# Seven-product down projections for twelve of the 22 chunks in both FFNs of a hybrid encoder block

## The chip, the cores and the metric

The kernel runs on one core of a Trainium2 chip. The metric is device time in microseconds, the median of several runs. In the profile PE is the matmul engine, PEld its weight load, DVE, ACT and POOL are the vector, scalar and GpSimd engines, and SP issues most DMAs.

## What is computed

One encoder layer on 512 tokens of width 1024, in float32: an FFN, a mixer of two attention groups, and a second FFN, each with RMS norms around it. The change touches the FFNs alone:

```python
def swiglu(h, w_gu, w_down):
    gate, up = jnp.split(h @ w_gu, 2, axis=-1)
    return (jax.nn.silu(gate) * up) @ w_down

f = swiglu(rms_norm(h, ffn1_pre_g[l]), ffn1_w_gu[l], ffn1_w_down[l])
h = h + 0.5 * rms_norm(f, ffn1_post_g[l])
...
f = swiglu(rms_norm(h, ffn2_pre_g[l]), ffn2_w_gu[l], ffn2_w_down[l])
h = h + 0.5 * rms_norm(f, ffn2_post_g[l])
```

The hidden width is 2816, which is 22 chunks of 128. `ffn1_w_down` is 2816 x 1024.

## The kernel before

Every float32 operand is split in two fp32r parts, a high one (an ACT copy) and a low one (a DVE or POOL subtraction): `split`, line 333. A product is three matmuls, high x high, high x low and low x high (`mm3`, line 351). The low part's subtraction has two inputs from SBUF.

`ffn` (line 392) has two stages. The first makes the gated hidden values chunk by chunk. Its first chunks are plain (`gate_up`); from chunk `direct` on, `winograd` (line 460) makes gate and up together by a form of seven products in place of eight, with operand sums on POOL and DVE (`operands`, line 434) and a recombination on DVE and ACT. It uses matmuls of 256 columns. Each chunk of 128 x 512 gated values goes to DRAM (`gd`).

The second stage is the down projection: out[token, 1024] is a sum over 22 chunks. The 512 tokens are four tiles of 128, and the 1024 output columns two halves, so the sums fill all eight PSUM banks of 128 x 512, bank 2n + hf. For each chunk `load_w` fetches 128 rows of `w_dn` (512 KB) and splits them, `load_gT` (line 530) fetches the chunk's gated values (256 KB) and splits them into a place of `slots`, and `down` (line 539) runs for each tile three matmuls of 512 columns into each of two banks: 24 matmuls per chunk. Chunks 0 and 1 are done two tiles at a time, chunks 2 to 17 in the loop at line 557, and the last four (`TAIL`) tile by tile, so that each tile's norm and residual addition (`on_tile`) run beside the next tile's matmuls. The four residual loads (`SP.dma_start(h[n], resid(n))`, lines 555 and 556) stand ahead of that loop. For the first FFN, tile n's work also issues what the mixer needs: `mid1` (line 703) and `after1` (line 710).

The order of all instructions on each engine is set by `Plan` (lines 47 to 239). It records every operation with the ranges that it reads and writes, places them in a list schedule by costs of its own, forwards and backwards several times, and emits the best order. `tc.keep_in_program_order` then holds it. This is why nearly every instruction of the profile stands at line 238.

The tile `m32` holds plain float32 data (loads, scratch `scr`, the residual `hall`); its name in the profile is `m`. The tile `memr` holds the split parts.

Of the kernel before, what the change touches and what calls it, by code (L numbers as in the profile page):

```python
# [15 lines left out]
ALU = mybir.AluOpType  # L16
AX = mybir.AxisListType

P = 128
D = 1024  # L20
S = 512
NT = S // P
KD = D // P
FF = 2816
NFC = FF // P
# [4 lines left out]
TAIL = 4  # L30
# [216 lines left out]
def hybrid_block(ctx, tc, A, out):  # L247
# [16 lines left out]
    def bank(i, n=512):  # L264
        return psum[:, i * 512 : i * 512 + n]
# [39 lines left out]
    def reg(o, n):  # L305
        assert R0 + o + n <= NCOL - N32
        return mem[:, R0 + o : R0 + o + n]
# [40 lines left out]
    def mm(ps, a, b, start, stop):  # L348
        return PE.matmul(ps, r_(a), r_(b), start=start, stop=stop, skip_group_check=True)
# [42 lines left out]
    def ffn(w_gu, w_dn, gpost, on_tile, L, first, resid, mid_tile=None, rs=None):  # L392
# [133 lines left out]

        slots, last_w = ([reg(o, 1024) for o in x] for x in (L["slots"], L["last_w"]))
        gT = {}

        def load_gT(c):  # L530
# [8 lines left out]
        def down(c, n, w, first, last, hfs=(0, 1)):  # L539
            t = slice(n * P, (n + 1) * P)  # L540
            for (a, b) in ((0, 0), (0, 1), (1, 0)):
                for hf in hfs:
                    mm(bank(2 * n + hf), gT[c][a][:, t], w[b][:, hf * 512 : hf * 512 + 512],
                       first and a + b == 0, last and a == 1)

        g = load_g(gpost)
# [4 lines left out]
        for ns in ((0, 1), (2, 3)):  # L551
            for c in range(2):
                for n in ns:
                    down(c, n, w01[c], c == 0, False)
        for n in range(NT):
            SP.dma_start(h[n], resid(n))
        for c in range(2, NFC - TAIL):
            w = load_w(w_dn[c * P : (c + 1) * P, :])
            load_gT(c)
            for n in range(NT):  # L560
                down(c, n, w, c == 0, False)
        ws = []
        for c in range(NFC - TAIL, NFC):
            ws.append(load_w(w_dn[c * P : (c + 1) * P, :], to=last_w if c == NFC - 1 else None))
            load_gT(c)
# [156 lines left out]
    def scale(k):  # L722
# [13 lines left out]
        "order": lambda c: 1 if c < 8 else (c + 1) % 2,  # L736
        "slots": [1024 * i for i in range(7)] + [8192 + 1024 * i for i in range(6)]
        + [26624 + 1024 * i for i in range(4)] + [7168] + [14336 + 1024 * i for i in range(4)],
        "last_w": (26624, 27648),
    }  # L740
# [416 lines left out]
    def after2(n, t):  # L1157
# [15 lines left out]
        "order": lambda c: c % 2,  # L1173
        "slots": [19456 + 1024 * i for i in range(7)] + [4096 + 1024 * i for i in range(15)],
        "last_w": (19456, 20480),
    }
# [70 lines left out]
```

## Time and profile before

| what | before |
|---|---|
| median of 3 runs | 946.56 us (946.36 to 946.84) |
| the profiled execution | 949.77 us |
| its span from first to last instruction | 948.0 us |
| PE busy | 937.1 us (99%) |
| DVE busy | 693.6 us (73%) |
| ACT busy | 477.9 us (50%) |
| POOL busy | 289.6 us (31%) |

The busy times are shares of the span. An engine's share is a mean over stages that differ: the gate and up stages, the mixer and the down stages each have their own.

### The profile page before, as it was taken

What the parts mean: (1) busy time and instruction counts of PE and PEld (TensorE: products, weight loads), DVE (VectorE), ACT (ScalarE), POOL (GpSimd) and SP (SyncE); (2) the same over time, 40 slices, a digit from 0 to 9 for tenths busy, and PEclk for the clock granted to TensorE, in tenths of its full rate; (3) what the DMA queues carried; (4) which work ended last, traced back from release to release, by engine and by line L of the source; (5) the groups of instructions that cost most, each with busy time, mean ns of one, the idle gap of its engine ahead of it and who ended that gap; (6) DMA issues with size and microseconds to landing.
All of it is one profiled execution on the core that took longest, in us unless ns stands there. A gap on an engine that the chain in (4) does not pass through costs nothing. (4 is left out here: it accounts for less than half of the span.)

```text
span 948.0 us, 15333 instructions
## 1 busy us (share of the span) xinstructions
PE 937.1 (99%) x5930; PEld 850.5 (90%) x5930; DVE 693.6 (73%) x977; ACT 477.9 (50%) x850; POOL 289.6 (31%) x233
## 2 busy tenths in 40 slices
PE   9999999999999999999999999999999999999996
PEld 8789999999888888889988888999999999988885
DVE  5799999998622376587687678999989899642224
ACT  5545455544521353588677767654445444432122
POOL 0005575660000013222452323227566672000000
PEclk9999999999999999999899999999999999999999
DMA  9634444449762356113371115254444337843312
GB/s 271 219 129 157 149 131 134 134 150 283 238 152 88 122 189 132 46 55 68 103 175 47 45 45 178 92 191 141 136 133 139 141 112 230 265 158 91 91 43 89
DMA packets 61897, 130.11 MB, mean 137 GB/s; under 512 B 21888, under 2 KB 23808, under 8 KB 61824
## 3 DMA queue, kind: packets, MB, share of 16 engines
q1 hardware_dynamic: 60672, 127.30, 43.0%
q0 software_dynamic: 1008, 1.84, 1.1%
q8 instruction: 46, 0.75, 0.3%
q14 instruction: 27, 0.22, 0.1%
q10 hardware_dynamic: 144, 0.00, 0.0%
HBM read 109.45 MB, written 17.83 MB: 134 GB/s over the span
## 5 line engine op out<-in xcount | busy, mean ns | idle before, releaser
L238 PE MATMUL psum<-memr 128*128 128x256 f32 (+2 forms) x5572 | 914.5, 324 | 0.4 <-ACT memr L238 0.2
L238 PEld LDWEIGHTS psum<-memr 128*128 128x128 f32 x5572 | 808.5, 191 | 78.6 <-ACT memr L238 2.1
L238 DVE TENSOR_TENSOR memr<-m,memr 128x1024 fp32r<-128x1024 f32 (+3 forms) x313 | 367.0, 1196 | 132.6 <-ACT memr L238 132.5
L238 POOL TENSOR_TENSOR m<-m 128x512 f32<-128x512 f32 (+5 forms) x193 | 252.1, 1321 | 567.6 <-DVE m L238 397.4
L238 ACT CAST memr<-m 128x1024 fp32r<-128x1024 f32 (+1 forms) x321 | 265.1, 841 | 277.2 <-PE psum L238 167.8
L238 DVE TENSOR_TENSOR m<-psum,m 128x512 f32<-128x512 f32 (+3 forms) x176 | 109.7, 625 | 36.0 <-ACT m L238 22.7
L238 DVE TENSOR_TENSOR memr<-psum,memr 128x512 fp32r<-128x512 f32 (+3 forms) x116 | 68.0, 603 | 24.8 <-ACT memr L238 23.8
L238 ACT CAST memr<-psum 128x512 fp32r<-128x512 f32 (+2 forms) x124 | 62.6, 524 | 41.8 <-PE psum L238 31.8
L238 PE MATMUL psum<-m 128*128 128x128 f32 (+1 forms) x358 | 59.3, 285 | 3.1 <-DVE m L238 3.1
L238 PEld LDWEIGHTS psum<-m 128*128 128x128 f32 x358 | 47.9, 162 | 11.1 <-DVE m L238 3.6
L238 ACT ACTIVATE m<-psum 128x256 f32<-128x256 f32 (+2 forms) x62 | 27.4, 444 | 53.5 <-PE psum L238 33.0
L238 ACT ACTIVATE m<-m 128x256 f32<-128x256 f32 (+3 forms) x80 | 36.9, 461 | 27.2 <-DVE m L238 26.9
L238 DVE TENSOR_TENSOR psum<-psum,m 128x512 f32<-128x512 f32 (+1 forms) x78 | 42.8, 571 | 6.4 <-PE psum L238 5.4
L238 ACT COPY m<-psum 128x256 f32<-128x256 f32 (+3 forms) x72 | 30.9, 432 | 24.6 <-PE psum L238 23.0
L238 DVE SCALAR_TENSOR_TENSOR m<-m 128x512 f32<-128x512 f32 (+1 forms) x36 | 33.7, 968 | 4.9 <-POOL m L238 4.3
L238 DVE TENSOR_TENSOR m<-m 128x512 f32<-128x512 f32 (+2 forms) x42 | 33.2, 799 | 0.7
L238 ACT ACTIVATE m<-psum,m 128x512 f32<-128x512 f32 x40 | 27.0, 688 | 10.3 <-DVE m L238 7.3
L238 ACT ACTIVATE memr<-m 128x512 fp32r<-128x512 f32 (+2 forms) x28 | 21.0, 760 | 13.2 <-DVE m L238 9.9
L238 POOL TENSOR_TENSOR memr<-m,memr 128x1024 fp32r<-128x1024 f32 x9 | 21.6, 2409 | 14.6 <-ACT memr L238 13.0
L238 POOL CAST memr<-memr 64x512 fp32r<-64x512 f32 x8 | 5.9, 740 | 51.4 <-DVE memr L238 51.4
L238 DVE TENSOR_SCALAR m<-m 128x1 f32<-128x1 f32 (+1 forms) x36 | 6.4, 179 | 20.6 <-ACT m L238 10.7
L238 DVE TENSOR_REDUCE m<-psum 128x1 f32<-128x512 f32 x32 | 21.2, 682 | 0.1
(24 smaller groups left out, 95.6 us busy)
## 6 DMA issues: line engine op xcount, KB each, us to landing
m<-in_ffn_w_gu SPq DMA_DIRECT2D x86, 512.0 KB
m<-in_ffn_w_down SPq DMA_DIRECT2D x44, 512.0 KB
gd<-m SPq DMA_DIRECT2D x44, 256.0 KB
m<-gd SPq DMA_DIRECT2D x44, 256.0 KB
m<-in_x SPq DMA_DIRECT2D x8, 512.0 KB
m<-in_w_qk SPq DMA_DIRECT2D x8, 512.0 KB
h<-m SPq DMA_DIRECT2D x8, 512.0 KB
m<-in_w_out SPq DMA_DIRECT2D x8, 512.0 KB
```

Of the source, the lines that this page charges most:

```text
L238: r = getattr(self.engines[eng], op)(*a, **k)
```

## The change

Chunks 3 to 8 and 12 to 17 of each FFN go two chunks and two token tiles at a time. With two chunks as the inner split, two tiles as rows and two column halves as columns, each such block is a 2 x 2 by 2 x 2 product, done with seven products in place of eight. Three pairs of chunks make a group (`down_pairs`).

- `weight_operands` makes the seven right-hand operands of a pair of chunks: four DVE subtractions of 128 x 512, then the split of seven 128 x 512 blocks (four ACT copies and four DVE subtractions).
- `gate_operands` makes the seven left-hand operands for two chunks and two tiles: two loads of 128 x 256, four POOL operations of 128 x 128, and splits of 384 and of 512 columns.
- The seven products of one token pair need seven banks (0 to 2 keep their running sums, 4 to 7 are fresh), and the two tiles' own four sums are the ones in banks 0 to 3. So the other token pair's four sums are copied to SBUF (`keep`, which is the residual's place `hall`), the first pair runs, eight DVE additions recombine it into `keep` and the other pair's sums come back into banks 0 to 3; then the second pair runs and is recombined in PSUM, and the first pair's sums go into banks 4 to 7. The table `at` notes that the two pairs have changed places.
- The residual loads move behind the loop, since `hall` is in use until then. The places of the split gated values (`slots`) become few and are reused, where before each chunk had its own.

```diff
-        slots, last_w = ([reg(o, 1024) for o in x] for x in (L["slots"], L["last_w"]))
+        plain = [c for c in range(NFC - TAIL) if not any(p <= c < p + 6 for p in L["pairs"])]
+        slots = {c: reg(L["slots"][0] + i % 3 * 1024, 1024) for i, c in enumerate(plain)}
+        slots |= {c: reg(L["slots"][1] + (c - NFC + TAIL) * 1024, 1024) for c in range(NFC - TAIL, NFC)}
         gT = {}
+        at = {(n, hf): 2 * n + hf for n in range(NT) for hf in range(2)}
...
-                    mm(bank(2 * n + hf), gT[c][a][:, t], w[b][:, hf * 512 : hf * 512 + 512],
+                    mm(bank(at[n, hf]), gT[c][a][:, t], w[b][:, hf * 512 : hf * 512 + 512],
...
+        keep = [hall[:, 512 * i : 512 * i + 512] for i in range(8)]
+        raw_w = Ring([scr[:, 1024 * i : 1024 * i + 1024] for i in range(3)])
+
+        def weight_operands(i, c):
+
+            m = reg(L["w_at"][i], 7168)
+            r0 = raw_w.get()
+            r1 = raws.get() if i == 1 else raw_w.get()
+            for r, k in ((r0, c), (r1, c + 1)):
+                SP.dma_start(r, w_dn[k * P : (k + 1) * P, :])
+            b11, b12, b21, b22 = r0[:, :512], r0[:, 512:], r1[:, :512], r1[:, 512:]
+            part = lambda i, j: (m[:, 512 * i : 512 * j], m[:, 3584 + 512 * i : 3584 + 512 * j])
+            DVE.tensor_tensor(b12, b12, b11, ALU.subtract)
+            split(*part(0, 1), b11)
+            split(*part(1, 3), r1)
+            DVE.tensor_tensor(b22, b22, b12, ALU.subtract)
+            DVE.tensor_tensor(b11, b22, b11, ALU.subtract)
+            DVE.tensor_tensor(b21, b21, b22, ALU.subtract)
+            split(*part(3, 5), r0)
+            split(*part(5, 7), r1)
+            return {k: part(i, i + 1) for i, k in enumerate(("11", "21", "22", "T3", "T1", "T4", "T2"))}
+
+        def gate_operands(i, c, n):
+
+            m = [reg(o, 1024) for o in L["g_at"][i]]
+            raw = half_g.get()
+            for k in range(2):
+                SP.dma_start(raw[:, 256 - 256 * k : 512 - 256 * k], gdr[c + k][:, n * P : (n + 2) * P])
+            a12, a22, a11, a21 = (raw[:, P * k : P * k + P] for k in range(4))
+            part = lambda i, j: (m[0][:, P * i : P * j], m[1][:, P * i : P * j])
+            split(*part(0, 3), raw[:, :384])
+            POOL.tensor_tensor(a21, a11, a21, ALU.subtract)
+            POOL.tensor_tensor(a22, a22, a21, ALU.subtract)
+            POOL.tensor_tensor(a12, a12, a22, ALU.subtract)
+            POOL.tensor_tensor(a11, a22, a11, ALU.add)
+            split(*part(3, 7), raw)
+            return {k: part(i, i + 1) for i, k in enumerate(("12", "22", "11", "S4", "S2", "S1", "S3"))}
+
+        def down_pairs(c0):
+
+
+            x, y = sorted((at[n, 0] // 4, n) for n in (0, 2))
+            x, y = x[1], y[1]
+            gs = Ring(range(4))
+            W = [weight_operands(i, c0 + 2 * i) for i in range(3)]
+            for i in range(4):
+                ACT.copy(keep[i], bank(4 + i))
+            for n in (x, y):
+                for i in range(3):
+                    G = gate_operands(gs.get(), c0 + 2 * i, n)
+                    for b, l, r in ((0, "12", "21"), (1, "S4", "22"), (2, "22", "T4"), (4, "11", "11"),
+                                    (5, "S2", "T2"), (6, "S3", "T3"), (7, "S1", "T1")):
+                        mm3(bank(b), G[l], W[i][r], b > 3 and i == 0, i == 2)
+                to = [keep[6], keep[0], keep[1], keep[2]] if n == x else [bank(i) for i in range(4)]
+                p1, u2, u3, u4, u5 = (keep[i] for i in (4, 5, 7, 4, 5))
+                back = (lambda i: ACT.copy(bank(i), keep[i])) if n == x else lambda i: None
+                add = lambda o, a, b: DVE.tensor_tensor(o, a, b, ALU.add)
+                ACT.copy(p1, bank(4))
+                add(u2, bank(5), p1)
+                add(to[0], bank(0), p1)
+                back(0)
+                add(u3, bank(6), u2)
+                add(u4, bank(7), u2)
+                add(to[1], bank(1), u4)
+                back(1)
+                add(u5, bank(7), u3)
+                add(to[2], bank(2), u3)
+                back(2)
+                add(to[3], bank(3), u5)
+                back(3)
+            for i, k in enumerate((6, 0, 1, 2)):
+                ACT.copy(bank(4 + i), keep[k])
+            for i in range(4):
+                at[y + i // 2, i % 2], at[x + i // 2, i % 2] = i, 4 + i
...
-        for n in range(NT):
-            SP.dma_start(h[n], resid(n))
-        for c in range(2, NFC - TAIL):
+        c = 2
+        while c < NFC - TAIL:
+            if c in L["pairs"]:
+                down_pairs(c)
+                c += 6
+                continue
             w = load_w(w_dn[c * P : (c + 1) * P, :])
             load_gT(c)
             for n in range(NT):
                 down(c, n, w, c == 0, False)
+            c += 1
+        for n in range(NT):
+            SP.dma_start(h[n], resid(n))
         ws = []
         for c in range(NFC - TAIL, NFC):
-            ws.append(load_w(w_dn[c * P : (c + 1) * P, :], to=last_w if c == NFC - 1 else None))
+            ws.append(load_w(w_dn[c * P : (c + 1) * P, :]))
...
+        "pairs": (3, 12), "w_at": (9216, 16384, 23552), "g_at": [(3072 + 2048 * i, 4096 + 2048 * i) for i in range(3)] + [(0, 1024)],
+        "slots": (0, 12288),
...
+        "pairs": (3, 12), "w_at": (0, 7168, 23552), "g_at": ((14336, 15360), (16384, 17408), (18432, 22528), (19456, 20480)),
+        "slots": (19456, 0),
```

Three places of the planned order show it. The first is PE in the first FFN's down stage, before (-) and now (+); the 128 x 128 rows are transposes of the next stage.

```order
 L238 MATMUL psum<-memr 128x256 x1344
-L238 MATMUL psum<-memr 128x512 x492
-L238 MATMUL psum<-m_63 128x128 x8
-L238 MATMUL psum<-memr 128x512 x24
+L238 MATMUL psum<-memr 128x512 x460
+L238 MATMUL psum<-m_63 128x128 x8
+L238 MATMUL psum<-memr 128x512 x20
```

36 matmuls of 512 columns are gone (in the second FFN one run of 528 becomes 492), and the first transposes stand four matmuls nearer the end of the stage.

The second is DVE in the same stage. Before, between the last gate and up chunk and the first tile's norm there are only low parts (`memr<-m,memr`): 512 columns for gated values, 1024 for weights.

```order
L238 TENSOR_TENSOR memr<-m_63,memr 128x1024
L238 TENSOR_TENSOR memr<-m_63,memr 128x512 x4
L238 TENSOR_TENSOR memr<-m_63,memr 128x1024
L238 TENSOR_TENSOR memr<-m_63,memr 128x512 x3
L238 TENSOR_TENSOR memr<-m_63,memr 128x1024 x17
L238 TENSOR_TENSOR m_63<-psum,m_63 128x512
```

Now the first group's weight operands stand there, subtractions in `m` and low parts of three sets in one run:

```order
L238 TENSOR_TENSOR m_63<-m_63 128x512 x4
L238 TENSOR_TENSOR memr<-m_63,memr 128x1024 x2
L238 TENSOR_TENSOR memr<-m_63,memr 128x512
L238 TENSOR_TENSOR m_63<-m_63 128x512 x3
L238 TENSOR_TENSOR memr<-m_63,memr 128x384
L238 TENSOR_TENSOR memr<-m_63,memr 128x1024 x2
L238 TENSOR_TENSOR m_63<-m_63 128x512
L238 TENSOR_TENSOR memr<-m_63,memr 128x512
L238 TENSOR_TENSOR memr<-m_63,memr 128x1024
L238 TENSOR_TENSOR m_63<-m_63 128x512 x3
L238 TENSOR_TENSOR memr<-m_63,memr 128x512
L238 TENSOR_TENSOR memr<-m_63,memr 128x1024 x2
```

The addition from PSUM that begins the first recombination follows these rows directly.

The third is POOL between the first FFN's gate and up stage (its 128 x 512 rows) and the mixer (64 x 128).

```order
 L238 TENSOR_TENSOR m_63<-m_63 128x512 x56
-L238 TENSOR_TENSOR m_63<-m_63 128x1 x5
+L238 TENSOR_TENSOR m_63<-m_63 128x128 x48
+L238 TENSOR_TENSOR m_63<-m_63 128x1 x8
+L238 TENSOR_TENSOR m_63<-m_63 64x128 x3
+L238 TENSOR_TENSOR m_63<-m_63 128x256
```

The 48 operations of 128 x 128 are the two groups' gate operands; POOL had none in the down stage.

## Rows read from the trace of the kernel before

**Rows 1.** The page's busy line; then PE's waits: us, times, longest.

```profile
PE 937.1 (99%) x5930; PEld 850.5 (90%) x5930; DVE 693.6 (73%) x977; ACT 477.9 (50%) x850; POOL 289.6 (31%) x233
...
PE psum L238 <- DVE m L238: 3.1, 4, 1.1
```

**Rows 2.** Busy time by stretch, clock, DMA: gate and up twice, down.

```profile
core 0: us, PE busy (x) PEld busy (x) DVE busy (x) ACT busy (x) POOL busy (x), PEclk, DMA share, GB/s
100.00:200.00 100.00, 100.00 (x835) 100.00 (x835) 97.74 (x102) 51.60 (x81) 64.98 (x42) 1.00 0.41 135
640.00:800.00 160.00, 160.00 (x1336) 160.00 (x1335) 148.25 (x164) 76.93 (x128) 102.61 (x64) 1.00 0.44 144
840.00:900.00 60.00, 60.00 (x266) 49.70 (x265) 14.19 (x12) 11.55 (x12) 0.00 (x0) 1.00 0.32 97
```

**Rows 3.** Groups by shape, 840 to 900 us, down: busy, mean ns, idle before.

```profile
L238 PE MATMUL psum<-memr 128*128 128x512 f32 x266 | 60.5, 389 | 0.0
...
L238 DVE TENSOR_TENSOR memr<-m,memr 128x1024 fp32r<-128x1024 f32 x11 | 13.5, 1226 | 45.2 <-ACT memr L238 45.2
...
L238 DVE TENSOR_TENSOR memr<-m,memr 128x512 fp32r<-128x512 f32 x1 | 0.7, 694 | 0.4 <-ACT memr L238 0.4
```

**Rows 4.** Timeline, gate and up: start, length, engine; DVE back to back.

```profile
194.69 0.68 DVE L238 TENSOR_TENSOR m<-psum,m 128x512 f32<-128x512 f32 x1
...
195.29 1.21 DVE L238 TENSOR_TENSOR memr<-m,memr 128x1024 fp32r<-128x1024 f32 x1
...
196.43 1.02 DVE L238 TENSOR_TENSOR psum<-psum,m 128x512 f32<-128x512 f32 x2
```

**Rows 5.** Groups by shape, whole run, DVE: subtraction inside SBUF.

```profile
L238 DVE TENSOR_TENSOR m<-m 128x512 f32<-128x512 f32 x26 | 17.6, 687 | 0.5
```

**Rows 6.** Groups by shape, whole run, POOL.

```profile
L238 POOL TENSOR_TENSOR m<-m 128x256 f32<-128x256 f32 x20 | 17.9, 898 | 42.0 <-DVE m L238 40.7 <-ACT memr L238 1.0
L238 POOL TENSOR_TENSOR m<-m 64x128 f32<-64x128 f32 x16 | 7.9, 494 | 3.4 <-DVE m L238 2.7
```

**Rows 7.** Groups by shape, DVE, 100 to 200, then 640 to 800 us.

```profile
L238 DVE TENSOR_TENSOR memr<-m,memr 128x512 fp32r<-128x512 f32 x32 | 45.5, 1473 | 0.0
L238 DVE TENSOR_TENSOR memr<-m,memr 128x1024 fp32r<-128x1024 f32 x20 | 27.7, 1386 | 0.0
L238 DVE TENSOR_TENSOR m<-psum,m 128x512 f32<-128x512 f32 x30 | 20.5, 682 | 2.3 <-ACT m L238 1.2
...
L238 DVE TENSOR_TENSOR memr<-m,memr 128x512 fp32r<-128x512 f32 x51 | 61.9, 1245 | 0.0
L238 DVE TENSOR_TENSOR memr<-m,memr 128x1024 fp32r<-128x1024 f32 x32 | 43.7, 1372 | 0.0
```

**Rows 8.** Groups by shape, whole run, ACT.

```profile
L238 ACT CAST memr<-m 128x1024 fp32r<-128x1024 f32 x164 | 170.0, 1047 | 189.8 <-PE psum L238 139.1 <-POOL m L238 19.8 <-DVE m L238 16.2
L238 ACT CAST memr<-m 128x512 fp32r<-128x512 f32 x152 | 93.3, 620 | 85.9 <-PE psum L238 27.2 <-POOL m L238 22.4 <-DMA m<-gd 15.4
...
L238 ACT ACTIVATE psum<-m 128x1024 f32<-128x1024 f32 x8 | 8.2, 1027 | 6.6 <-DMA m<-in_x 5.4 <-DVE m L238 1.1
L238 ACT COPY m<-psum 128x512 f32<-128x512 f32 x13 | 7.4, 586 | 1.4 <-PE psum L238 0.8 <-DVE memr L238 0.5
```

**Rows 9.** Busy by stretch (columns as in rows 2); PE's groups in 233 to 235.

```profile
215.00:230.00 15.00, 15.00 (x127) 15.00 (x126) 12.49 (x19) 6.31 (x12) 0.00 (x0) 1.00 1.01 285
320.00:346.00 26.00, 26.00 (x116) 21.52 (x116) 15.40 (x19) 11.88 (x18) 1.66 (x3) 1.00 0.59 201
...
L238 PE MATMUL psum<-memr 128*128 128x512 f32 x2 | 0.6, 397 | 0.0
```

**Rows 10.** Timeline, end of the first gate and up stage: its last addition.

```profile
236.17 0.69 DVE L238 TENSOR_TENSOR m<-psum,m 128x512 f32<-128x512 f32 x1 [0.51 <-ACT m L238]
```

**Rows 11.** Timeline, second down stage: a weight load, and a later copy.

```profile
832.47 0.33 SPq L238 DMA_DIRECT2D m<-in_ffn_w_down  x1
...
836.78 1.57 ACT L238 CAST memr<-m 128x512 fp32r<-128x512 f32 x2 [2.37 <-DMA m<-gd]
```

More of the change, by code (lines that the diff above doesn't have):

```diff
@@ L736, in hybrid_block @@
         "order": lambda c: 1 if c < 8 else (c + 1) % 2,
-        "slots": [1024 * i for i in range(7)] + [8192 + 1024 * i for i in range(6)]
-        + [26624 + 1024 * i for i in range(4)] + [7168] + [14336 + 1024 * i for i in range(4)],
-        "last_w": (26624, 27648),
+        "pairs": (3, 12), "w_at": (9216, 16384, 23552), "g_at": [(3072 + 2048 * i, 4096 + 2048 * i) for i in range(3)] + [(0, 1024)],
+        "slots": (0, 12288),
     }
@@ L1173, in hybrid_block @@
         "order": lambda c: c % 2,
-        "slots": [19456 + 1024 * i for i in range(7)] + [4096 + 1024 * i for i in range(15)],
-        "last_w": (19456, 20480),
+        "pairs": (3, 12), "w_at": (0, 7168, 23552), "g_at": ((14336, 15360), (16384, 17408), (18432, 22528), (19456, 20480)),
+        "slots": (19456, 0),
     }
```

## The prediction

> **What bounds the kernel now.** I began with the page's busy line and the waits. PE is busy for 937.1 of 948.0 us, and its longest waits for another engine are four for DVE, 3.1 us in all [rows 1]. So a matmul that is taken away is worth its full time, as long as the other engines keep up. Next come the stretches [rows 2]: in the gate and up stage (100 to 200 us, 640 to 800 us) PE and DVE are both nearly full, in the down stage (840 to 900 us) PE is full while DVE works 14.19 us of 60 and POOL not at all. The change spends that free DVE time to save PE time. The question is whether there is enough of it in the right places.
>
> **What it removes.** For two chunks and two token tiles, eight products of three matmuls become seven. Six chunks are 144 matmuls of 512 columns, now 126; there are two such groups in each FFN, so 4 x 18 = 72 go, as the order of PE shows (492 to 460 plus 24 to 20 in FFN 1, 528 to 492 in FFN 2). In the down stage 266 of them fill 60.00 us [rows 2, 3], 0.2256 us each: 72 x 0.2256 = **16.2 us less**. The granted clock is 1.00 in these stretches, so none of it is slow-clock time.
>
> **What it adds to DVE.** DVE's own durations overlap at their ends: starts at 194.69, 195.29 and 196.43 us follow a 512-column and a 1024-column operation by 0.60 and 1.14 us [rows 4], where the rows give 0.68 and 1.21. I count 0.60 and 1.14, and the same 0.60 for a 512-column subtraction (0.687) and for an addition from PSUM (0.682) [rows 5, 7]. From 0.60 to 1.14 is 0.54 for 512 columns more, so a 384-column low part comes to 0.60 - 0.54 / 4 = 0.47.
> One group of six chunks then costs DVE: three weight sets, each four subtractions, one 512-column and three 1024-column low parts, 5 x 0.60 + 3 x 1.14 = 6.42, so 19.3; six gate sets, 0.47 + 0.60 each, 6.4; two recombinations of eight additions, 16 x 0.60 = 9.6. Together 35.3 us, where the six plain chunks cost 6 x (1.14 + 0.60) = 10.4. PE spends 126 x 0.2256 = 28.4 us on the group, so DVE is 6.9 us short within it.
> It must work ahead, in the three plain chunks that stand before each group (chunks 0 to 2 and 9 to 11): PE needs 72 x 0.2256 = 16.2 us there, DVE 3 x 1.74 = 5.2, which leaves 11.0. So each group with its three chunks ends **4.1 us** to the good, if nothing slows DVE. DVE is loaded to 40.5 of 44.6 us.
>
> **POOL against DVE.** Each group adds 24 subtractions and additions of 128x128 on POOL (the order shows 48 per FFN). No such row exists before: the nearest are 0.494 us for 64x128 and 0.898 us for 128x256 [rows 6]; I take 0.494, since those have the same columns, so 11.9 us of POOL per group. What that costs DVE is bounded by rows. In the gate and up stage a 512-column low part (two inputs from SBUF) takes 1.473 us beside POOL, where it takes 0.694 in the down stage without POOL; a 1024-column one 1.386 against 1.226. Operations that read PSUM stay at 0.682 [rows 3, 7]. Between 100 and 200 us DVE thus lost 32 x 0.779 + 20 x 0.160 = 28.1 us beside 64.98 us of POOL [rows 2], 0.43 us for each us of POOL; between 640 and 800 us 51 x 0.551 + 32 x 0.146 = 32.8 beside 102.61, 0.32. I take the middle, 0.37: 4.4 us per group against the 4.1 to the good, **0.3 us of PE's time per group**, 1.2 in all. The ends are 0 (POOL falls where DVE reads PSUM or idles: no loss) and 11.9 (all of POOL's time: 7.8 us per group).
> The Trainium skill, page "SBUF — State Buffer", section "Who interferes with whom", says that a DVE instruction with two SBUF inputs and a GpSimd instruction that reads SBUF exclude each other for their whole length, and that one with at most one SBUF input is free of it. The trace agrees on the kinds (1.473 beside POOL, 0.682 from PSUM). By that rule taken to its end all 11.9 us would fall on DVE, which is the slower rival below.
>
> **Handovers.** Each group now has two points where PE follows closely on DVE: the last weight set in the first half, and the change from the first token pair to the second. There DVE adds into SBUF, ACT puts the other pair's sum into the freed bank, then PE may go on: 0.60 + about 0.6. ACT's copy from PSUM is 0.586; into PSUM there is only a 1024-column row, 1.027, so I bound the 512-column copy by 0.51 and 0.62 [rows 8]. The order lets PE first fill banks 4 to 6 and bank 0 of the second pair, some 12 to 16 matmuls or 2.7 to 3.6 us, while the last chain (three additions and a copy, 2.4 us) runs. So I expect these to be mostly hidden. Where PE waited for DVE before, it was 3.1 / 4 = 0.78 us each [rows 1]; I charge one such wait per group, **3.1 us** (bounds: none, and two per group, 6.2).
>
> **What costs nothing, and its cover.** ACT: per group 3 x (0.620 + 3 x 1.047) + 6 x 1.13 + 14 x 0.6 = 26.3 us [rows 8], below PE's 28.4 and with the plain chunks beside it. SP: 24 more gate loads of 128 KB with rows half as long; no more bytes. The residual loads (four of 512 KB) move from the start of the down stage, where DMA stood at a share of 1.01, to after the second group [rows 9]. In FFN 1 they meet the loads of the next stage, at 0.59 and 201 GB/s between 320 and 346 us; 2 MB over 26 us adds 81 GB/s, just the 285 that the same chip moved earlier. I cost it at nothing; if a load is late, the first tile's residual addition and with it the transposes behind it wait.
>
> **Sum.** -16.2 + 1.2 + 3.1 = **-11.9 us**. The profiled execution took 949.77 us (span 948.0), 0.34% above the median of 946.56; the terms are differences, so against the median: 946.56 - 11.9 = **934.7 us**.
>
> **Rivals.**
> *No price at all.* DVE's lead holds everywhere and every handover is hidden: 946.56 - 16.2 = 930.4 us. For it: DVE is idle for 45.8 of 60 us now. Against it: the balance has only 4.1 us in 44.6.
> *DVE becomes the bound (the slower one).* POOL's 128x128 operations come one by one into DVE's densest stretch, and each holds up a two-input operation for its full length: 7.8 us short per group, 4 x 7.8 + 3.1 = 34.3, and 946.56 - 16.2 + 34.3 = 964.7 us. The point that decides is where 47.6 us of POOL times the loss per us, less 4 x 4.1, plus 3.1, reaches 16.2: 0.62 us lost per us of POOL. Rows show 0.32 and 0.43, but in a stage in which DVE has other work to put between. A loss of 0.43 to 0.62 gives 937 to 947 us.
> *Weights come late.* The first group's chunks 3 to 5 are loaded into the scratch that the last gate and up recombination still uses. That ends with the addition at 236.17 us, some 2.5 us after the first 512-column matmul (two in 233 to 235) [rows 9, 10]. A weight load was issued at 832.47 us, and the copy that waited for the gate load next behind it began at 836.78, 4.3 us for 768 KB [rows 11]. With the gate write ahead of them I expect the first two chunks after some 8 us, the three sets by 8 + 19.3 = 27.3, and PE wants the last of them after 130 matmuls, 29.3 us: 2.0 us in hand. Four us later on DMA would cost 2.0 us per FFN, 938.7 us; with the residual loads late as well, about 942.
> *The change doesn't act.* PE's order has exactly 72 fewer matmuls and PE is the bound, so I give this nothing of its own.
>
> **Chances.** Forecast (931.5 to 938.5) 0.45; no price 0.22; partly DVE-bound (to 947) 0.13; late loads 0.08; DVE-bound and slower 0.12. A measurement of this kernel can tell about 0.2%, 1.9 us, from no change. Faster: 0.45 + 0.22 + 0.08 and most of the 0.13, 0.86; within 0.2%: 0.03; slower: 0.11. The range runs from 930.0 to 943.0: it takes in the forecast, nearly all of "no price", the better half of "partly DVE-bound" and most of "late loads", 0.80 together.
>
> **What would show it.** Right: PE has 72 fewer 512-column matmuls at the same 0.2256 us; DVE in the down stage is at about 90%; PE's waits for DVE grow from 3.1 us to some 7, in spells under 1 us, in both FFNs alike. The POOL step is wrong if the 512-column two-input operations of the groups show well above 0.8 us in the mean and PE waits in spells of several us for weight operands. The handover step is wrong if PE waits behind ACT's copies into PSUM. The load step is wrong if ACT or DVE wait for weight loads at a group's start, or the transposes after FFN 1 come late. A time above 943 us would mean that DVE, not PE, sets the pace of the down stage.

## The result, and the profile after

| | before | after | forecast |
|---|---|---|---|
| median | 946.70 us (4 runs, 946.36 to 948.11) | 934.39 us (4 runs, 932.50 to 934.53) | 934.7 us |
| profiled execution | 949.77 us | 934.53 us | |
| its span | 948.0 us | 932.8 us | |

The ratio is 0.9863, with a 95% interval of 0.9846 to 0.9880: faster by 12.3 us. On another chip (run `after_again` below) it was 936.09 against 947.62 us, a ratio of 0.9876 (0.9853 to 0.9899).

The page's busy line of after, and then PE's waits (us, times, longest), which answer to [rows 1]:

```profile
PE 920.2 (99%) x5858; PEld 835.6 (90%) x5858; DVE 797.7 (86%) x1137; ACT 535.2 (57%) x954; POOL 380.6 (41%) x329
```

```profile
PE psum L238 <- DVE m L238: 3.1, 4, 1.1
PE psum L238 <- ACT m L238: 1.2, 1, 1.2
PE psum L238 <- ACT memr L238: 0.6, 2, 0.4
PE psum L238 <- DVE memr L238: 0.3, 1, 0.3
```

PE has 5930 - 5858 = 72 matmuls less. DVE has 104 us more work and POOL 91 us more, but PE's waits for DVE's `m` are the same 3.1 us. New are one wait of 1.2 us behind ACT and one of 0.38 us (in the 0.6), in the second FFN's first group (its timeline):

```profile
841.21 11.17 PE L238 MATMUL psum<-memr 128*128 128x512 f32 x46 [0.38 <-ACT memr L238]
```

Busy time by stretch, columns as in [rows 2], of both down stages of after:

```profile
234.70:324.70 90.00, 90.00 (x399) 74.48 (x398) 81.41 (x107) 55.22 (x83) 26.25 (x35) 1.00 0.44 142
809.00:900.00 91.00, 90.58 (x412) 74.80 (x411) 83.31 (x110) 55.44 (x83) 33.13 (x43) 1.00 0.41 133
```

DVE is busy for 81.41 of 90 and 83.31 of 91 us, 90 to 92%, with PE's clock granted at 1.00 (2.4 GHz). Now the shapes in the second down stage of after (811 to 900 us), where [rows 3, 5, 6] had 694 ns for the 512-column low part, 687 for the subtraction and 494 for POOL's nearest shape:

```profile
L238 DVE TENSOR_TENSOR m<-m 128x512 f32<-128x512 f32 x24 | 16.9, 727 | 0.6 <-DMA m<-in_ffn_w_down 0.2
L238 DVE TENSOR_TENSOR memr<-m,memr 128x512 fp32r<-128x512 f32 x23 | 16.5, 729 | 0.8 <-ACT memr L238 0.8
L238 DVE TENSOR_TENSOR m<-psum,m 128x512 f32<-128x512 f32 x21 | 13.9, 684 | 1.3 <-ACT m L238 0.9
L238 DVE TENSOR_TENSOR memr<-m,memr 128x384 fp32r<-128x384 f32 x11 | 7.5, 695 | 0.0
...
L238 POOL TENSOR_TENSOR m<-m 128x128 f32<-128x128 f32 x41 | 32.4, 808 | 48.7 <-issue 15.7 <-DMA m<-gd 14.6 <-ACT m L238 13.2
```

DVE's two-input operations are a few per cent longer; POOL's take 0.81 us each.

**Where the time went.** I cut each profiled execution at marks on PE. D1 runs from the first 512-column matmul of the first down stage to the transposes behind the mixer's first run of 122 matmuls (before: 234.58 to 395.66 us). The mixer runs from there to the transposes that open the second FFN (607.30). F2 runs from those to the last long piece of the chain of waits, "issue" (936.82). The marks of after, from PE's timeline and the chain:

```profile
389.02 0.38 PE L238 MATMUL psum<-m 128*128 128x128 f32 x2
...
599.09 1.07 PE L238 MATMUL psum<-m 128*128 128x128 f32 x8 [0.68 <-DVE m L238]
```

```profile
841.21 8.09 PE psum L238 x34
849.34 70.60 PE psum L238 x310
921.58 4.85 issue
```

The first down stage of after starts at 234.70, so D1 is 154.32, the mixer 210.07 and F2 322.49 us. All runs by the same cut (one profiled execution each), with the medians:

| run | D1 | mixer | F2 | median |
|---|---|---|---|---|
| before | 161.08 | 211.64 | 329.52 | 946.70 |
| after | 154.32 | 210.07 | 322.49 | 934.39 |
| after_again | 157.56 | 210.16 | 322.21 | 936.09 |
| e1_minus72 | 152.91 | 210.00 | 321.35 | 931.91 |
| e2_ffn1_only | 154.35 | 210.03 | 329.51 | 940.74 |
| e3_ffn2_only | 161.07 | 210.11 | 323.79 | 941.35 |
| e4_no_pool | 155.20 | 209.94 | 324.36 | 937.32 |
| p1_no_pool | 153.86 | 208.63 | 321.35 | 931.97 |
| p2_no_resid1 | 153.49 | 209.91 | 322.05 | 934.18 |
| p3_dve_twice | 179.61 | 208.64 | 343.80 | 976.65 |
| f2_later2 | 154.83 | 210.13 | 322.19 | 934.64 |
| e9_earlier1 | 156.43 | 209.74 | 322.06 | 936.47 |
| g1_both | 157.25 | 210.48 | 322.41 | 937.85 |
| e7_adjacent | 168.77 | 208.65 | 334.76 | 957.40 |

Between the two profiled executions D1 lost 6.76 us and F2 7.03, 13.8 together. The mixer, which the change doesn't touch, lost another 1.57: the profiled execution of before had a longer spell of lower clock there (last section). So the spans differ by 15.2 us and the medians by 12.3. Three executions of after's order in the second FFN (after, after_again, p2) give F2 within 0.44 us. After's order in the first FFN ran in after, after_again, e2 and f2, where D1 is 154.32 to 157.56 us, so D1 has to be read with its waits. The chips differ far less: e2 repeats before's F2, and e3 its D1, to 0.01 us on another one.

### The profile page after: what moved, and what is told of

The parts are those of the page before. It is cut to its first block, busy times and chain, and to the rows that moved or that the text cites. A ratio compares the mean times of both kernels' runs of the same rounds, so it can differ in the third digit from the quotient of the medians.

```text
span 932.8 us, 15683 instructions
## 1 busy us (share of the span) xinstructions
PE 920.2 (99%) x5858; PEld 835.6 (90%) x5858; DVE 797.7 (86%) x1137; ACT 535.2 (57%) x954; POOL 380.6 (41%) x329
## 5 line engine op out<-in xcount | busy, mean ns | idle before, releaser
L238 PE MATMUL psum<-memr 128*128 128x256 f32 (+3 forms) x5500 | 898.4, 323 | 0.9 <-ACT memr L238 0.6
L238 PEld LDWEIGHTS psum<-memr 128*128 128x128 f32 x5500 | 794.4, 191 | 77.3 <-ACT memr L238 3.1
L238 POOL TENSOR_TENSOR m<-m 128x512 f32<-128x512 f32 (+5 forms) x289 | 343.1, 1203 | 477.9 <-DVE m L238 186.5
L238 DVE TENSOR_TENSOR memr<-m,memr 128x512 fp32r<-128x512 f32 (+3 forms) x361 | 402.3, 1144 | 20.0 <-ACT memr L238 17.5
L238 ACT CAST memr<-m 128x1024 fp32r<-128x1024 f32 (+2 forms) x369 | 292.9, 818 | 203.1 <-PE psum L238 70.1
L238 DVE TENSOR_TENSOR m<-psum,m 128x512 f32<-128x512 f32 (+4 forms) x224 | 141.6, 638 | 37.5 <-ACT m L238 23.7
L238 DVE TENSOR_TENSOR m<-m 128x512 f32<-128x512 f32 (+2 forms) x90 | 67.2, 764 | 1.5 <-DMA m<-in_ffn_w_down 0.2
L238 ACT COPY m<-psum 128x512 f32<-128x512 f32 (+3 forms) x96 | 43.8, 471 | 28.9 <-PE psum L238 27.6
L238 DVE TENSOR_TENSOR psum<-psum,m 128x256 f32<-128x256 f32 (+1 forms) x94 | 55.2, 594 | 2.7 <-ACT m L238 0.4
L238 ACT ACTIVATE m<-m 128x256 f32<-128x256 f32 (+3 forms) x80 | 36.8, 461 | 20.7 <-DVE m L238 20.5
L238 ACT COPY psum<-m 128x512 f32<-128x512 f32 x32 | 18.9, 590 | 16.4 <-DVE m L238 16.2
```

Of the source, the lines that this page charges most:

```text
L238: r = getattr(self.engines[eng], op)(*a, **k)
```

## The experiments

The twelve runs were made in three sets, each on one chip with its own runs of before (medians 947.02, 947.96 and 947.62 us).

**e1_minus72: the matmuls alone.** Before, with 72 matmuls left out:

```diff
             for (a, b) in ((0, 0), (0, 1), (1, 0)):
                 for hf in hfs:
+                    if n == 3 and hf == 1 and (3 <= c < 9 or 12 <= c < 18):
+                        continue
```

> The kernel before, with 72 matmuls of 512 columns left out (in both FFNs the three of the last token tile's second column half in chunks 3 to 8 and 12 to 17, so that part of the down projection is missing) and nothing added. It prices the removed matmuls alone. Theory (each is worth its full 0.2256 us, as PE is the bound): 8.1 us less in each down stage, 16.2 in all, about 930.5 us. Rival (the engines beside PE hold part of it back, so that the removal is worth no more than the change showed): 12 to 13 us less, about 934.5 us.

Measured: 931.91 us, a ratio of 0.9832 (0.9815 to 0.9850). D1 and F2 are each 8.17 us shorter, 36 x 0.2256 = 8.1 with nothing held back. The medians differ by 15.1 us, with 2.4 us of spread among that set's runs of before. The theory holds. These two lengths, 152.91 and 321.35, are the floor against which the change's price is read: after pays 1.41 us in D1 and 1.14 in F2.

Where it pays shows when the starts of the 512-column matmuls of both traces are laid side by side, counted from the first of each down stage. In the first FFN the matmul behind the second group starts at 89.81 us in after and at 89.79 in e1: both groups are free, and all but 0.02 us of the 1.41 comes behind them. In the second FFN the two are level for 28 us; the matmul behind the first group starts at 46.04 against 44.91 us, and nothing is lost after that. So three of the four groups cost PE nothing. In after_again the picture is the same; in e2, with after's order in the first FFN, the first group there loses 0.66 us.

**e2_ffn1_only and e3_ffn2_only: one FFN at a time.** The other FFN runs as before, with its old places and its residual loads ahead of the loop (here for the second):

```diff
-        "pairs": (3, 12), "w_at": (0, 7168, 23552), "g_at": ((14336, 15360), (16384, 17408), (18432, 22528), (19456, 20480)),
-        "slots": (19456, 0),
+        "pairs": (),
+        "slots": [19456 + 1024 * i for i in range(7)] + [4096 + 1024 * i for i in range(15)],
+        "last_w": (19456, 20480),
```

> The change in the first FFN alone; the second FFN as in the kernel before. From the traces of before and after the first FFN's part is -8.1 for 36 matmuls, +1.2 for the wait of the transposes behind it, so -6.9, about 939.8 us. The forecast's own terms give -8.1 + 0.6 (POOL) + 1.55 (handovers) = -5.95, about 940.7 us. If the two FFNs' shares are not independent (the mixer's clock differs because of what goes before), the mixer between them differs in length from the one of before by more than 0.3 us at a granted clock that is the same.

> The change in the second FFN alone; the first FFN as in the kernel before. From the traces the second FFN's part is -8.1 + 0.4 (PE's wait for the first group's weight operands) + some 0.7 not yet placed, so -7.0, about 939.7 us; the first FFN's wait for the transposes must be absent. If the price there came from what the first FFN left behind (late loads, order), this run shows -8.1, about 938.6 us.

Measured: 940.74 us for the first FFN alone, ratio 0.9937 (0.9913 to 0.9961), D1 6.73 us shorter and F2 as before. The second alone: 941.35, ratio 0.9932 (0.9916 to 0.9948), D1 as before and F2 5.73 us shorter, not 7.0. For the first FFN the two expected sums, 939.8 and 940.7 us, both lie within its four runs (939.68 to 944.68), and D1's 6.73 is nearer to the 6.9 from the traces than to the forecast's 5.95. The 5.73 us of e3 was in neither of its theories. The planner sees a different program and gives the second FFN another order, in which two of the first group's 1024-column low parts come later on DVE; PE's timeline of e3:

```profile
841.70 5.51 PE L238 MATMUL psum<-memr 128*128 128x512 f32 x23 [0.23 <-ACT memr L238]
847.42 0.51 PE L238 MATMUL psum<-memr 128*128 128x512 f32 x1 [0.21 <-ACT memr L238]
848.37 0.96 PE L238 MATMUL psum<-memr 128*128 128x512 f32 x3 [0.44 <-ACT memr L238]
```

The FFNs' shares are independent as far as D1 goes. All of the 2.44 us that e3's F2 has over e1's is lost by the end of the second FFN's first group, so that is a place where an order costs a microsecond more or less.

**e4_no_pool, and p1_no_pool with the order held.** e4 leaves POOL's four operations per gate set out of the program. p1 lets the planner order the whole program and then doesn't issue them:

```diff
-        for i in sorted(range(n), key=lambda i: (best[1][i], i)):
+        for i in sorted([i for i in range(n) for _ in range(self.times.get(i, 1))], key=lambda i: (best[1][i], i)):
...
             POOL.tensor_tensor(a11, a22, a11, ALU.add)
+            plan.times.update({len(plan.ops) - 1 - j: 0 for j in range(4)})
```

> The changed kernel without the four POOL operations of each gate set (the sums of gated values are left out, so that four of the seven products have a wrong left operand). Forecast's POOL step: 0.37 us of DVE lost per us of POOL, 1.2 us of PE's time in all, so 1.2 us less than the change; slower rival of the forecast: up to 7.8 per group, far more. Theory from the after trace (POOL's operations wait, at 0.80 us each, and DVE loses 0.04 to 0.05 us per two-input operation, which its slack covers): the same time within 0.5 us, DVE's 512-column low parts back at 0.69 us from 0.73 to 0.74.

> The changed kernel with the order of every other instruction held as it is and the four POOL operations of each gate set not issued (four of the seven products thus have a wrong left operand). The forecast's POOL step (0.37 us of DVE lost per us of POOL, 1.2 us of PE's time): down stages 0.6 us shorter each, 933.2 us against the change's 934.4. The slower rival's full lock: more than that. Theory from the trace of after (the lock makes POOL wait, 0.80 us an operation where 0.49 was expected, and DVE has slack except at the second FFN's first group): first FFN's down stage unchanged within 0.2 us, second at most 0.5 us shorter, DVE's 512-column low parts back from 0.73 to about 0.69 us.

Measured: e4 937.32 us, slower than the change with less work, D1 155.20 and F2 324.36. Its order is another one, as in e3, so it says nothing of POOL. p1: 931.97 us, ratio 0.9834 (0.9816 to 0.9853), D1 0.46 us shorter than after and F2 1.14 shorter. The 0.46 us is not shown to be POOL's. Matmul by matmul p1 and after are level in D1 up to the second set of transposes, where after waits 1.20 us and p1 0.75, and that wait varies between executions of one order (p2, below). PE's timeline of p1:

```profile
344.38 1.06 PE L238 MATMUL psum<-m 128*128 128x128 f32 x8 [0.75 <-issue]
```

F2's marks in p1, from PE's timeline and the chain of waits:

```profile
596.21 1.06 PE L238 MATMUL psum<-m 128*128 128x128 f32 x8 [0.67 <-DVE m L238]
```

```profile
917.56 4.85 issue
```

That is 321.35 us, the very length of e1, which has none of the change's added work. So in the second FFN POOL is the whole price (1.14 us against this profile of after, 0.7 against the shortest of the three with its order), and banks, copies and recombinations cost PE nothing. Part of that price goes through the loads: at the start of the down stage a 384-column low part of DVE takes 0.82 us beside POOL and 0.55 in p1, and the first group's second weight load is issued 3.02 us into the stage and 2.65 in p1. DVE's shapes of p1 in 811 to 900 us:

```profile
L238 DVE TENSOR_TENSOR memr<-m,memr 128x512 fp32r<-128x512 f32 x25 | 16.7, 686 | 0.5 <-ACT memr L238 0.5
L238 DVE TENSOR_TENSOR m<-m 128x512 f32<-128x512 f32 x24 | 15.9, 688 | 1.5 <-DMA m<-in_ffn_w_down 1.2
...
L238 DVE TENSOR_TENSOR memr<-m,memr 128x384 fp32r<-128x384 f32 x9 | 4.8, 552 | 0.0
```

Beside POOL these were 729, 727 and 695 ns, and 1024-column low parts 1260 against 1221. With after's counts DVE loses 23 x 0.043 + 24 x 0.039 + 11 x 0.143 + 24 x 0.039 = 4.4 us to 32.4 us of POOL, 0.14 us for each; the same sum in the first FFN (236 to 325 us) gives 4.2 to 25.5, 0.16. My theory was right for the first FFN (unchanged within 0.2 us, the wait at the transposes set aside) and took the second at half its size (0.5 at most).

DVE in the first down stage of p1, by stretch, and the group that most of its idle time from 244 to 324 us stands in front of:

```profile
234.00:324.00 90.00, 90.00 (x399) 74.50 (x398) 77.57 (x107) 55.49 (x83) 0.00 (x0) 1.00 0.44 142
244.00:324.00 80.00, 80.00 (x355) 66.24 (x354) 73.64 (x102) 50.59 (x76) 0.00 (x0) 1.00 0.41 134
...
L238 DVE TENSOR_TENSOR m<-psum,m 128x512 f32<-128x512 f32 x22 | 14.7, 687 | 5.0 <-ACT m L238 3.3 <-PE psum L238 1.1
```

**p2_no_resid1: the residual loads.** Order held, the first FFN's four residual loads not issued:

```diff
             SP.dma_start(h[n], resid(n))
+            if rs is not None:
+                plan.times[len(plan.ops) - 1] = 0
```

> The changed kernel with the order held and the first FFN's four residual loads not issued (its residual is thus missing). Forecast: costed at nothing, so the same time, 934.4 us. Theory from the trace of after: with them, 342 to 346 us of DMA are full, the mixer's weight load lands late, ACT waits 2.37 us for it and PE's transposes 1.20 us behind ACT. Without them that wait is gone and the first FFN's down stage is 1.2 to 1.4 us shorter, about 933.1 us.

Measured: 934.18 us, ratio 0.9853 (0.9838 to 0.9867), too near for a median to tell. D1 is 0.83 us shorter, and PE's wait at the transposes falls from 1.20 us to 0.38:

```profile
344.66 1.06 PE L238 MATMUL psum<-m 128*128 128x128 f32 x8 [0.38 <-issue]
```

The chain of after, from its timeline:

```profile
327.95 1.88 SPq L238 DMA_DIRECT2D m<-in_x  x3
...
339.53 1.05 ACT L238 CAST memr<-m 128x1024 fp32r<-128x1024 f32 x1 [2.37 <-DMA m<-in_w_v]
...
344.44 1.28 DVE L238 SCALAR_TENSOR_TENSOR m<-m 128x1024 f32<-128x1024 f32 x1 [0.44 <-POOL m L238]
...
345.83 1.06 PE L238 MATMUL psum<-m 128*128 128x128 f32 x8 [1.20 <-ACT m L238]
```

and the DMA in that stretch, before, after and in p2, from the busy times by stretch (columns as in [rows 2]):

```profile
340.00:345.00 5.00, 5.00 (x24) 4.13 (x23) 4.33 (x8) 2.41 (x6) 0.56 (x1) 1.00 0.78 295
```

```profile
340.00:345.00 5.00, 4.62 (x21) 3.48 (x19) 3.81 (x7) 4.03 (x10) 1.46 (x1) 1.00 1.05 265
```

```profile
340.00:345.00 5.00, 4.62 (x22) 3.56 (x21) 4.54 (x8) 2.83 (x7) 1.69 (x2) 1.00 0.59 179
```

With the residual loads DMA is full and the mixer's weight load late; ACT, whose work goes in the planned order, stands 2.37 us in front of that weight's cast, with the next tile's norm behind it. The theory holds for the wait, at 0.83 us and not the 1.2 to 1.4 expected; the 0.38 us left is not explained. This is one execution, but the shortest wait of six: with the residual loads the same order waits 0.61 us in e2, 0.75 in p1, 1.20 in after, 1.69 in f2 and 2.64 in after_again.

**p3_dve_twice: is there DVE time to spare?** Order held, three low parts of each weight set made twice:

```diff
             split(*part(1, 3), r1)
+            plan.times[len(plan.ops) - 1] = 2
...
             split(*part(3, 5), r0)
+            plan.times[len(plan.ops) - 1] = 2
             split(*part(5, 7), r1)
+            plan.times[len(plan.ops) - 1] = 2
```

> The changed kernel with the order held and each 1024-column low part of the weight sets made twice, 9 more DVE operations of about 1.14 us per group, 10.3 us per group, 41 us in all. The forecast's balance (DVE loaded to 40.5 of 44.6 us per group with its three plain chunks): 10.3 - 4.1 = 6.2 us lost per group, 25 in all, about 959 us; by DVE's idle time in the trace of after (8.6 us of the first FFN's 90.4, 7.7 of the second's 91): 20.6 - 8 = 12.5 per FFN, the same. Rival (DVE's work is hidden anyway and the balance was never tight, as no wait of PE for the groups' operands in the first FFN suggests): under 5 us lost in all, below 940 us.

Measured: 976.65 us, ratio 1.0308 (1.0271 to 1.0345). 18 x 1.14 = 20.5 us of DVE per FFN made D1 25.3 us longer and F2 21.3. Neither number holds: nothing of the added work was hidden. The stretch from 245 us to about the end of the first FFN's second group, in after and then in p3:

```profile
245.00:325.00 80.00, 80.00 (x355) 66.18 (x354) 77.68 (x102) 50.62 (x76) 25.52 (x33) 1.00 0.42 134
```

```profile
245.00:346.00 101.00, 89.47 (x357) 69.24 (x356) 98.20 (x120) 51.06 (x76) 27.45 (x33) 0.93 0.35 109
```

With 18 operations and 20.5 us of DVE more, nearly the same matmuls take 21 us longer, and DVE is busy for 97% in both. The rest of D1's 25.3 us comes behind the groups, in waits at the transposes (1.72 and 2.56 us) and lower clock. Two lines of PE's waits over the whole run, and a stretch behind one wait:

```profile
PE psum L238 <- DVE memr L238: 15.5, 13, 3.4
...
PE psum L238 <- issue: 4.3, 2, 2.6
...
860.00:865.00 5.00, 5.00 (x12) 3.88 (x13) 4.93 (x8) 3.35 (x4) 0.00 (x0) 0.50 0.28 107
```

After a wait of 2.64 us PE runs 12 matmuls in 5 us at a granted clock of 0.50 (1.2 GHz), where 22 fit at 1.00 (2.4 GHz).

**f2_later2, e9_earlier1, g1_both: other places for the groups.**

```diff
-        "pairs": (3, 12), "w_at": (0, 7168, 23552), "g_at": ((14336, 15360), (16384, 17408), (18432, 22528), (19456, 20480)),
+        "pairs": (4, 12), "w_at": (0, 7168, 23552), "g_at": ((14336, 15360), (16384, 17408), (18432, 22528), (19456, 20480)),
```

e9 has (3, 11) in the first FFN instead, g1 both.

> The changed kernel with the second FFN's first group one chunk later (chunks 4 to 9 in place of 3 to 8), so that its weight loads, which wait for the last gate and up recombination's scratch, have a whole chunk (24 x 0.2256 = 5.4 us) more ahead of the first use, while the second group has one plain chunk less ahead of it. Theory (late weight loads cost that group 1.1 us): the second FFN's down stage 1.0 to 1.1 us shorter, about 933.3 us. Rival (the second group needs its three plain chunks for DVE's lead: 40.5 of 44.6 us with three, 38.8 of 39.2 with two): no gain, or up to 1 us more, 934.4 to 935.4 us.

> The first FFN's second group one chunk earlier (chunks 11 to 16 in place of 12 to 17), so that the residual's place is free, and its four loads can start, 5.4 us earlier; only two plain chunks stand between the groups. Theory (the residual loads crowd out the mixer's weight load and cost 0.8 us): the wait of the transposes falls below 0.5 us, the first FFN's down stage 0.8 us shorter, about 933.5 us. Rival (DVE has no time to spare, as doubling its low parts cost their full time, so one plain chunk less before a group costs 24 x 0.2256 - 3 x 1.14 / 2, some 1.7 to 3.7 us): about 936 to 938 us.

> First FFN's second group one chunk earlier (11 to 16) and second FFN's first group one chunk later (4 to 9). If both theories hold: 0.8 + 0.3 us less than the change, about 933.3 us. If a group needs three plain chunks ahead of it: the first FFN's part as in the run with that alone, the second FFN's 0.3 us shorter as in the run with that alone.

Measured: f2 934.64 us, ratio 0.9877 (0.9846 to 0.9907). The wait of 0.38 us at 841 us is gone, yet F2 is 322.19 us, inside the spread of the unchanged order: the rival (no gain) holds. e9: 936.47, ratio 0.9885 (0.9868 to 0.9902). The transposes no longer wait, but two plain chunks don't feed the second group; PE's timeline of e9:

```profile
293.32 2.37 PE L238 MATMUL psum<-memr 128*128 128x512 f32 x9 [1.50 <-DVE memr L238]
296.06 45.11 PE L238 MATMUL psum<-memr 128*128 128x512 f32 x195 [0.38 <-DVE memr L238]
```

DVE had worked from 274.87 to 295.3 us with no pause above 0.11 us. D1 is 156.43; the rival holds. g1: 937.85, ratio 0.9899 (0.9883 to 0.9916); its D1 of 157.25 and F2 of 322.41 us are those of e9 and f2 within 0.9 us. None is faster than the change.

**e7_adjacent: no plain chunks between the groups.**

In both tables, here that of the second:

```diff
-        "pairs": (3, 12), "w_at": (0, 7168, 23552), "g_at": ((14336, 15360), (16384, 17408), (18432, 22528), (19456, 20480)),
+        "pairs": (3, 9), "w_at": (0, 7168, 23552), "g_at": ((14336, 15360), (16384, 17408), (18432, 22528), (19456, 20480)),
```

> Both FFNs with the groups next to each other (chunks 3 to 8 and 9 to 14), no plain chunks between and three more behind. The forecast's balance: a group by itself leaves DVE 35.3 - 28.4 = 6.9 us short, so the second group of each FFN costs 6.9 us less what the first left over (0 to 4.1): 3 to 7 us per FFN, 940 to 948 us. Rival (the working ahead is not what hides the operands, the places of the weight sets set the order, as they are taken until the group before ends): under 1 us, 934 to 936 us, and the residual loads, free 16 us earlier, give 0.8 back.

Measured: 957.40 us, ratio 1.0110 (1.0088 to 1.0132): slower than before. D1 is 14.5 us longer than after's and F2 12.3. PE's timeline of e7, at the second group of each FFN:

```profile
291.12 47.84 PE L238 MATMUL psum<-memr 128*128 128x512 f32 x201 [6.62 <-DVE memr L238]
...
882.96 68.58 PE L238 MATMUL psum<-memr 128*128 128x512 f32 x288 [5.90 <-DVE memr L238]
```

The direction is the forecast's: the chunks ahead of a group hide its operands. The size is about two to five times the 3 to 7 us that its balance gives. The waits named are 6.62 and 5.90 us; the rest is smaller waits and clock (0.79 in 291 to 300 us).

**after_again: the change itself once more.**

> The changed kernel itself once more, beside the variants on one chip: 934.4 us within 1 us. By stage, if the prices found so far repeat: first FFN's down stage 154.3 us with a wait of PE's transposes of 1.0 to 1.4 us, second FFN from its first transposes to the end 322.0 to 322.5 us.

Measured: 936.09 us (933.38 to 937.90). F2 repeats, 322.21 us. D1 does not, 157.56 against 154.32; the lines of its timeline that answer to after's 339.53 and 345.83:

```profile
341.49 1.05 ACT L238 CAST memr<-m 128x1024 fp32r<-128x1024 f32 x1 [3.66 <-DMA m<-in_w_v]
...
347.80 1.23 PE L238 MATMUL psum<-m 128*128 128x128 f32 x8 [2.64 <-issue]
```

The same chain, with the weight 1.3 us later still, PE waits 2.64 us, and from 350 to 352 us its clock is granted at 0.51. That is 1.44 us more of waiting than in after; the rest of the 3.24 us goes with the lower clock. The wait at these transposes thus varies from one execution to the next, and so does what the residual loads cost.

## Why the forecast was right, and which of its terms were not

The sum was -11.9 us, the medians differ by 12.3 on one chip and 11.5 on the other. The price in the sum was 1.2 + 3.1 = 4.3 us. By stage it is 1.41 + 1.14 = 2.55 us in the profile of after and 4.65 + 0.86 = 5.5 us in that of after_again. It falls at the transposes behind the first FFN, where the sum had nothing, and in the second FFN's first group; the other three groups, with 3.2 us in the sum, cost nothing. So the saving was understood, and that the price came out so near is in part luck. Term by term:

- **Matmuls, -16.2.** Right: e1 gives 8.17 us per FFN.
- **DVE's load, 40.5 us per group.** Right as a load: 77.57 us busy of 90 without POOL (p1, 234 to 324 us), 38.8 per group, and 40.7 with it.
- **"4.1 us to the good".** Wrong in what it was worth, and the step that failed most. The balance took all of DVE's time beside the plain chunks for usable. In after DVE idles for 8.59 of 90 us in the first FFN, and 5.98 of them are one wait at the stage's start. ACT, then DVE, from the timeline:

```profile
241.28 1.46 ACT L238 CAST memr<-m 128x384 fp32r<-128x384 f32 x2 [3.74 <-PE psum L238]
...
242.77 1.23 DVE L238 TENSOR_TENSOR memr<-m,memr 128x1024 fp32r<-128x1024 f32 x1 [5.98 <-ACT memr L238]
```

By the profile ACT stands in front of a cast of gated values until PE releases it, and the weights' cast that DVE needs comes next in ACT's order. Behind that wait p1 idles for 6.36 us (244 to 324 us), 5.0 of them in front of additions from PSUM. That time took up POOL's 4.2 us in the first FFN, at no cost to PE, but it is no room for weight operands: p3's 20.5 us came through whole. The change fits by a margin of about nothing.
- **POOL, 1.2 us.** The size was about right (0.7 to 1.1 us by p1), the place was not: 0.3 us in each of four groups was forecast, and all of it came in one. DVE loses 0.15 us for each us of POOL, not 0.37, as POOL does most of the waiting (last section).
- **Handovers, 3.1 us.** Wrong: nothing. p1 holds every handover and is level with e1 behind its second group in both FFNs. PE never waits behind a copy into PSUM in after.
- **Residual loads, costed at nothing.** Wrong: 0.83 us by p2, and 2.64 us of wait where it went worse (after_again). The forecast compared bytes with a rate once reached, 285 GB/s; with them the DMA is at a share of 1.05 at 265 GB/s. The sign it named, transposes after FFN 1 late, is what came.
- **Late weights.** The rival of 2 us per FFN came as a wait of DVE, which was its other sign, but hardly as a price. In the second FFN of after one load of the first set took 6.27 us, from the chain of waits:

```profile
815.53 6.27 DMA m<-in_ffn_w_down
```

DVE stood still for 3.81 us behind it (at 822.96, last section), so that group runs with little lead, and it is there that POOL costs 1.14 us. p1 has a wait of 3.09 us at the same place and loses nothing.

One slip in the working has no effect: ACT's terms add up to 26.5 us, not 26.3.

So 3.1 for handovers stood where the wait at the transposes belonged; the total was right with a term at the wrong place. DVE at about 90%, a sign that the forecast gave for itself, came; PE's waits for DVE growing to 7 us did not. DVE as the bound, the slower rival, did not come, but p3 and e7 show how near it was: three more DVE operations in each weight set, or the three plain chunks moved away, and the kernel is slower than before.

Open is what F2 waits for in f2. Its 0.84 us over e1 come in steps of about 0.1 us, half of them in the first group, each too short for the list of waits. Open are also the last 0.38 us of wait in p2, whether the wait at 242 us would go with more places for gated values, and whether loading the residual of the last two tiles later, when DMA is free again, would win back D1's wait; the last two were not tried.

## What to carry to other kernels

A matmul saved on a full PE was worth its whole duration here, but pay for it with another engine's idle time only after asking where that time lies: this DVE was 90% busy, and the other 10%, spent waiting for casts and for sums, had no room for operands. Look for the price of a change where loads were moved to as well: a load that is put beside others can hold up a third engine whose order is fixed. And when a planner sets the order, hold the order while one suspect is taken out: e4, with less work and a new order, ran 5 us slower than p1.

## What was not expected of the hardware

**POOL yields more than DVE.** Of after's 96 POOL operations of 128x128, the 32 that no DVE operation with two SBUF inputs overlaps took 0.45 to 0.47 us each; the mean of all is 0.76. One took 0.52 us where it had begun before DVE's next two-input operation (an earlier one was just ending), and one 1.52 us where DVE's had begun 0.02 us earlier. From the timeline of after, first two back to back with nothing in their way:

```profile
307.97 0.88 POOL L238 TENSOR_TENSOR m<-m 128x128 f32<-128x128 f32 x2
...
818.07 0.52 POOL L238 TENSOR_TENSOR m<-m 128x128 f32<-128x128 f32 x1 [2.30 <-DMA m<-gd]
818.29 0.85 DVE L238 TENSOR_TENSOR memr<-m,memr 128x512 fp32r<-128x512 f32 x1
...
822.96 1.22 DVE L238 TENSOR_TENSOR memr<-m,memr 128x1024 fp32r<-128x1024 f32 x1 [3.81 <-ACT memr L238]
822.98 1.52 POOL L238 TENSOR_TENSOR m<-m 128x128 f32<-128x128 f32 x1 [4.39 <-DMA m<-gd]
```

In the 0.52 us case DVE's low part took 0.85 us, where it has 0.686 without POOL; in the other DVE's 1.22 us is what p1 shows without POOL (1.221). In the second down stage POOL's operations are in the mean 0.3 us longer than the 0.49 forecast, and DVE's 0.04 to 0.14 us. The Trainium skill, page "SBUF — State Buffer", section "Who interferes with whom", says that a DVE instruction with two SBUF inputs contends with a GpSimd instruction that reads SBUF, that the port pair they share is an exclusive lock, and that issue order decides who blocks. These lines agree on who blocks; on the length not quite, as the blocked POOL operation ends 0.32 us after DVE's, less than the 0.45 to 0.47 that such an operation takes with nothing in its way. The forecast's slower rival put all of POOL's time on DVE; the runs put most of the blocking on POOL.

**The clock falls after waits of about a microsecond, and not always.** In the mixer PE waits 0.98 us for DVE at 466 us, and then (before, columns as in [rows 2]; a clock of 0.50 is the lower of two levels, 1.2 GHz, and 1.00 the upper, 2.4 GHz):

```profile
466.00:470.00 4.00, 3.37 (x18) 3.19 (x18) 2.72 (x14) 2.68 (x4) 3.47 (x3) 0.66 0.16 65
470.00:480.00 10.00, 10.00 (x41) 8.23 (x41) 6.96 (x11) 5.14 (x10) 5.89 (x6) 0.79 0.59 177
```

After had the same wait (0.95 us), and 0.72 over the next 6 us, then full; p1 had it too and stayed at 1.00, and so did f2 behind its 1.69 us at the transposes. The mixer took 211.64, 210.07 and 208.63 us accordingly, though p1 issues after's mixer in after's order: steps of 1.5 us between executions, not between kernels. That is why lengths by stage tell here what medians can't.
